# A hybrid trunk layer on one core: the state-space projection as three dense passes behind the scan

## The chip, the cores and the metric

One core of one Trainium2 chip runs the whole program in one launch. The metric is the device time in microseconds. The engines are TensorE (PE), VectorE (DVE), ScalarE (ACT), GpSimd (POOL) and SyncE (SP), which issues nearly all DMAs, in its own order. The kernel before took 2487.5 us as the median of 3 runs.

## The reference

One layer with two sub-layers runs for a prompt of 1024 tokens and for a sample group of 8 single tokens that bring caches and states; D = 1024. All numbers are float32. Cut to what matters:

```python
mod = silu(c) @ w_ada + b_ada                      # six adaLN vectors
h = rmsnorm(x) * (1 + sc1) + sh1
q, k, v, z, xbc, dt_raw, gates = split(h @ w_in)   # 3 x 768, 2048, 4096, 32, 2048 columns
attn = dilated_window_attention(q, k, v, rel_bias, caches)  # 3 groups of 4 heads of 64, merged: 256 columns
xs, B, C = split(silu(causal_conv(xbc)))           # 8 groups of 4 heads; state 128
y = chunked_scan(xs, dt, A, B, C, state) + d_skip * xs      # chunks of 128 tokens
y = y * silu(z)                                    # 2048 columns
y = y * rsqrt(mean over each group of 256 (y * y) + eps) * ssd_norm_g
g_attn, g_ssd = split(sigmoid(gates))
merged = g_attn * (attn @ w_o_attn) + g_ssd * (y @ w_o_ssd)
x = x + g1 * (merged @ w_out)
x = x + g2 * (relu(rmsnorm2(x) @ w_up) ** 2 @ w_down)       # 4096 hidden
y = rmsnorm(x)
```

The updated key and value buffers, the conv tails and the scan states of both token groups are outputs too.

## The kernel before

**Dense jobs.** The tokens (1024 + 8) lie along the free axis in three chunks of 384, 384 and 264. A `Dense` job makes 128 output columns for all three: for a chunk it runs 3 matmuls for each 128 rows of the weight (L142 to L144: high part by high, high by low, low by high), so 24 for K = 1024, into one of three `mm` PSUM buffers, and then calls an eviction. Weights come by DMA on SP (`load_raw`, L81), ACT casts the high part (L97), POOL subtracts the low one (L98), one job ahead.

**Sides.** Everything else is written as generators in a list `sides`. `run(jobs, pace)` goes on by `pace` generator steps for each chunk of a dense job (`pump`), and `rest(n)` makes a generator stay away for n dense steps. The order on PE is the order in which this program writes it; the other engines' order follows from a scheduler. `ck` tiles (19 of 384 and 10 of 264 columns) hold the scan's inputs; a dense step that finds too few free (`live`, `gated`, `CKB`) pumps the generators further first, without dense work.

**Stages.** The prologue (to about 112 us) makes the adaLN vectors (class `Mod`, L258), the transposed input (`mx` generators, L377, L382) and the first jobs' first chunks (`first_`). Attention's jobs run to about 490 us, with `bias_side` (L440 to L443: the position bias of each of the 12 heads, spread over 128 partitions by a matmul, stored to `rep_d` and read back as `bias`) and `decode_attn` (the sample tokens; values L663, transposes L674). The scan runs to about 1500 us: for each of 8 groups two `z` jobs and four `x` jobs, beside three generators of the group before (`ssd_sides`): `decode` (the sample states, L879 to L884), `chunks` and `finish_`. Of 8 chunks of 128 tokens, `load` fetches decays to `ar` (L897) and `er` (L905), `prep` transposes (L908 to L911) and scales (L916 to L926, on DVE, ACT and POOL), `state` multiplies into the state (L932), `out` makes y (L947, L951, L958). `finish_` takes a token chunk of 384: `sums` gates y by z (L969) and sums squares (L283), `rstd` is a chain of ten small DVE operations (to L233), `norm` spreads it by transposes (L982), multiplies (L985) and splits y into high and low parts, and then `project` multiplies the group's 256 columns of y with `w_o_ssd`:

```python
for f in range(8):
    ...
    for ci, (t0, nt) in enumerate(CH):
        ps = ps_mm()
        ...
        if gi == 0:
            A.copy(sacc[f][:, t0:t0 + nt], ps[:, :nt])
        else:
            V.tensor_tensor(sacc[f][:, t0:t0 + nt], ps[:, :nt], sacc[f][:, t0:t0 + nt], op=OP.add)
```

with six matmuls (L1007 to L1009) and one eviction (L1013) for a chunk. Behind the scan 16 jobs make the gates (`ga_job` to SBUF, `gs_job` multiplied into `sacc`) beside `merge` (attention's groups), 8 `oa_job`s multiply attention with `w_o_attn` (K = 256, 6 matmuls a chunk) and add both branches (L1277 makes the low part), 8 `wo_job`s apply `w_out`, and the MLP fills 1750 to 2481 us.

Of the kernel before, what the change touches and what calls it, by code (L numbers as in the profile page):

```python
# [40 lines left out]
def _trunk(ctx, tc, nc, I, O):  # L41
# [42 lines left out]
    def load_w(src, r0, kt, c0, n, side=False, into=None, raw=None):  # L84
# [128 lines left out]
    dsel = consts.tile([128, 16, 17], F32, name="dsel")  # L213

    att_d = dram.tile([3, 2, NT, 132], F32, name="att_d")
    xT_d = dram.tile([8, 128, NT], F32, name="xT_d")
    rep_d = dram.tile([12, 128, 384], F32, name="rep_d")
    qkv_d = dram.tile([3, 8, 768], F32, name="qkv_d")
    bc_d = dram.tile([8, 2, 8, 128], F32, name="bc_d")
    ac_d = dram.tile([2, 32, 1024], F32, name="ac_d")  # L220

# [13 lines left out]
    class Mod:  # L235
# [10 lines left out]
        def steps(self, slow=False):  # L246
            m = self.pool.tile([128, 512], F32, name="m4", tag="m4", bufs=1)
# [8 lines left out]
            for k in range(8):  # L256
# [6 lines left out]
                else:  # L263
                    yield
            V.tensor_copy(m[:, :256], ps[:, :256])
# [13 lines left out]
    def rstd_cols(sq, scale, eps, pool):  # L279

        ps = ps_()
        for i in range(3):
            T.matmul(ps[:, i:i + 1], sq[:, i * 128:(i + 1) * 128], ones, start=True, stop=True)  # L283
        r = pool.tile([128, 3, 3], F32, name="rstd", tag="rstd", bufs=2)
        V.tensor_scalar(r[:, 1], ps[:, :3], scale, eps, op0=OP.mult, op1=OP.add)
# [19 lines left out]
    WADA = 3  # L305
# [53 lines left out]
    def make_x(ci):  # L359
# [21 lines left out]
        for i, j in enumerate(js):  # L381
            T.transpose(rb[:, i * 128:(i + 1) * 128], rs[:, 0, j:j + 1].to_broadcast([128, 128]), ident)  # L382
        for k in range(8):
            x = xn[k, ci] = p0.tile([128, nt], F32, name="xn", tag=f"xn{ci}", bufs=8)
# [42 lines left out]
    def bias_side():  # L427
# [4 lines left out]
        for g in range(3):  # L432
            ohs.append(dp.tile([33, 384], F32, name="oh", tag="oh", bufs=2))
# [1150 lines left out]
```

## Time and profile before

| | |
|---|---|
| median of 3 runs (lowest, highest) | 2487.5 us (2484.05, 2489.03) |
| the profiled execution's own time | 2491.66 us |
| its span in the trace | 2489.9 us |
| mean granted clock of TensorE | 0.98 |
| PE busy | 2363.1 us, 95% |
| DVE, ACT, POOL busy | 1254.2, 866.6, 736.9 us |
| DMA | 254.75 MB, mean 102 GB/s |

The span goes from the first to the last instruction. Busy time is summed for each engine; a busy PE can still be slower than its best, since matmuls are pipelined and their ends are modelled. A wait is put down to the instruction that released it. PEclk is the clock that TensorE was granted, as a share of 2.4 GHz: 0.50 is 1.2 GHz.

### The profile page before, as it was taken

Reading aid. Unit: us, or ns where it says so; the run is one execution under the profiler, and the core shown is the slowest. Engines: PE = TensorE matmul, PEld = TensorE weight load, DVE = VectorE, ACT = ScalarE, POOL = GpSimd, SP = SyncE. Lnnn points to the kernel's source line nnn. Section 1 sums busy time; section 2 is a strip of 40 time slices with the busy share of each in tenths; the row PEclk is TensorE's granted clock in tenths of the full one; section 3 lists DMA queues with packets and bytes.
Section 4 is the critical chain, followed back from the end, with each engine's and each line's share of the span. In section 5 each row is a group of like instructions: output and inputs, shape, how many; then the busy total and the mean of one; then the engine's idle time right before and its main releaser. Section 6 shows DMA issues by size and latency. Waiting matters only on the chain.

```text
span 2489.9 us, 40907 instructions
## 1 busy us (share of the span) xinstructions
PE 2363.1 (95%) x15243; PEld 2245.5 (90%) x15243; DVE 1254.2 (50%) x3507; ACT 866.6 (35%) x2171; POOL 736.9 (30%) x699
## 2 busy tenths in 40 slices
PE   5999999999999999999999999989999999999998
PEld 3878898988999889989898999989999999999997
DVE  3443233677576767676767434345433333333336
ACT  4423333355543444434343312224321221221232
POOL 1112121244343434434343433343222222222230
PEclk8999999999999999999999999999999999999999
DMA  8254433343333333332333223121544544411111
GB/s 286 90 173 142 155 81 84 102 123 84 100 85 86 92 79 103 80 102 73 100 74 96 61 60 76 52 88 58 177 133 139 174 140 141 148 44 51 55 39 69
DMA packets 332482, 254.75 MB, mean 102 GB/s; under 512 B 21511, under 2 KB 323130, under 8 KB 326507
## 3 DMA queue, kind: packets, MB, share of 16 engines
q1 hardware_dynamic: 332282, 252.14, 34.8%
q8 instruction: 120, 1.97, 0.3%
q14 instruction: 80, 0.65, 0.1%
HBM read 224.50 MB, written 71.81 MB: 119 GB/s over the span
## 4 chain that ended last, share of the span: by engine, by line
PE 69%; DVE 10%; DMA 9%; issue 4%; POOL 4%; ACT 3%; SPq 1%; POOLq 0%; DVEq 0%; ACTq 0%
PE mm L142 19%; PE mm L143 19%; PE mm L144 19%; DVE ck L814 2%; DMA ar<-ac_d 2%; DMA bc<-bc_d 2%; POOL wlo L98 1%; DMA qb<-qkv_d 1%; PE ps L560 1%; DVE acc L1013 1%; DVE hst L879 1%; PE ps L951 1%; PE mm L1007 1%; DMA hst<-state_ssm 1%; PE mm L1009 1%
## 5 line engine op out<-in xcount | busy, mean ns | idle before, releaser
L142 PE MATMUL mm<-hh,whi 128*128 128x384 f32 (+4 forms) x2808 | 920.3, 328 | 7.0 <-DVE ck L814 4.7
L143 PE MATMUL mm<-hl,whi 128*128 128x384 f32 (+4 forms) x2808 | 902.2, 321 | 0.9 <-DMA xT_d<-xT 0.5
L144 PE MATMUL mm<-hh,wlo 128*128 128x384 f32 (+4 forms) x2808 | 902.2, 321 | 0.0
L98 POOL TENSOR_TENSOR wlo<-wraw,whi 128x512 fp32r<-128x512 f32 (+2 forms) x300 | 386.3, 1293 | 1022.2 <-ACT whi L97 982.6
L142 PEld LDWEIGHTS mm<-hh,whi 128*128 128x128 f32 (+1 forms) x2808 | 531.8, 189 | 14.9 <-issue 6.2
L143 PEld LDWEIGHTS mm<-hl,whi 128*128 128x128 f32 (+1 forms) x2808 | 531.0, 189 | 4.1 <-DVE hl L404 2.3
L144 PEld LDWEIGHTS mm<-hh,wlo 128*128 128x128 f32 (+1 forms) x2808 | 530.5, 189 | 1.2
L97 ACT CAST whi<-wraw 128x512 fp32r<-128x512 f32 (+2 forms) x300 | 181.4, 610 | 400.3 <-PE mm L143 318.7
L1287 DVE SCALAR_TENSOR_TENSOR acc<-mm,mod,acc 128x384 f32<-128x384 f32 (+1 forms) x216 | 123.5, 572 | 234.4 <-PE mm L144 233.4
L143 PE MATMUL mm<-dl,whi 128*128 128x384 f32 (+1 forms) x696 | 223.3, 321 | 0.0
L144 PE MATMUL mm<-dh,wlo 128*128 128x384 f32 (+1 forms) x696 | 222.3, 319 | 0.0
L142 PE MATMUL mm<-dh,whi 128*128 128x384 f32 (+1 forms) x696 | 222.3, 319 | 0.0
L814 DVE SCALAR_TENSOR_TENSOR ck<-mm,cwT,ck 128x384 f32<-128x384 f32 (+4 forms) x288 | 163.0, 567 | 66.6 <-ACT ck L810 62.9
L1374 DVE TENSOR_TENSOR r<-r 128x384 f32<-128x384 f32 (+1 forms) x96 | 69.5, 724 | 186.5 <-ACT r L1373 186.5
L1007 PE MATMUL mm<-ck,shi 128*128 128x384 f32 (+1 forms) x384 | 130.5, 340 | 23.1 <-DVE acc L1013 18.8
L926 POOL TENSOR_TENSOR ar<-ar,cb 128x512 f32<-128x512 f32 x64 | 83.4, 1303 | 161.5 <-DVE cb L921 117.4
L142 PEld LDWEIGHTS mm<-dh,whi 128*128 128x128 f32 x696 | 131.1, 188 | 0.0
L143 PEld LDWEIGHTS mm<-dl,whi 128*128 128x128 f32 x696 | 130.9, 188 | 0.0
L144 PEld LDWEIGHTS mm<-dh,wlo 128*128 128x128 f32 x696 | 130.8, 188 | 0.0
L1009 PE MATMUL mm<-ck,slo 128*128 128x384 f32 (+1 forms) x384 | 125.0, 326 | 0.6 <-POOL slo L98 0.4
L1008 PE MATMUL mm<-ck,shi 128*128 128x384 f32 (+1 forms) x384 | 124.8, 325 | 0.4 <-POOL ck L990 0.4
L923 ACT ACTIVATE ar<-ar,acs 128x128 f32<-128x128 f32 x256 | 85.3, 391 | 102.4 <-DMA ar<-ac_d 100.8
(335 smaller groups left out, 3399.8 us busy)
## 6 DMA issues: line engine op xcount, KB each, us to landing
wraw<-w_in SPq DMA_DIRECT2D x164, 256.0 KB
kv_g_sample<-cache_kv_g SPq DMA_DIRECT2D x144, 256.0 KB
wada<-w_ada SPq DMA_DIRECT2D x24, 1024.0 KB
ar<-ac_d SPq DMA_DIRECT2D x64, 256.0 KB
wraw<-w_up SPq DMA_DIRECT2D x64, 256.0 KB
wraw<-w_down SPq DMA_DIRECT2D x58, 256.0 KB
hst<-state_ssm SPq DMA_DIRECT2D x64, 128.0 KB
bc<-bc_d SPq DMA_DIRECT2D x32, 256.0 KB
```

Source lines behind the costliest of these rows:

```text
L97: A.copy(hi, raw)
L98: P.tensor_tensor(lo, raw, hi, op=OP.subtract)
L142: T.matmul(ps[:n, :m], wh, a, start=(k == 0), stop=False)
L143: T.matmul(ps[:n, :m], wh, b, start=False, stop=False)
L144: T.matmul(ps[:n, :m], wl, a, start=False, stop=(k == nk - 1))
L814: V.scalar_tensor_tensor(acc[:, o:n], ps[:, x0 + o - d:x0 + n - d], w[k], acc[:, o:n], op0=OP.mult, op1=OP.add)
L923: A.activation(ar[:, h, :], ar[:, h, :], AF.Relu, bias=acs[:, c, 4 * gi + h:4 * gi + h + 1], scale=-1.0)
L926: P.tensor_tensor(ar, ar, cb[:, None, :].to_broadcast([128, 4, 128]), op=OP.mult)
L1007: T.matmul(ps[:, :nt], hi[:, t, :], a, start=(t == 0), stop=False)
L1008: T.matmul(ps[:, :nt], hi[:, t, :], b, start=False, stop=False)
L1009: T.matmul(ps[:, :nt], lo[:, t, :], a, start=False, stop=(t == 1))
L1287: V.scalar_tensor_tensor(x[:, t0:t0 + n], ps[:, :n], gate[:, 0:1], x[:, t0:t0 + n], op0=OP.mult, op1=OP.add)
```

## The change

1. **Projection.** `project`, `rstd` and `norm` go from the scan. `gate(ci)` multiplies y by z, stores it to `y_d` (L979), and `sums` leaves the column sums in `ysum`. Behind the scan `yprep(q)` reads y back by quarters (512 columns), normalises (L1236, L1240) and splits it (L1243), and `os_job(q, f)` runs three passes of 8 jobs with K = 512, 512 and 1024; the first pass is evicted by ACT, the others add into `sacc` (L1308, L1311). In the last pass each job is followed by the `oa_job` of the same f.
2. **Chunks.** `state` and `out` of a chunk are a dense step apart, chunks are prepared three ahead and loaded four ahead, and `ar`, `er`, `xd`, `xw`, `bt`, `cb` and `hst` get more buffers.
3. **Gates.** The 16 gate jobs store their tanh to `tg_d` (L1153); five stand among the scan's `x` jobs, six at its end, five behind. `os_job` fetches the values back in its `pre`.
4. **Prologue.** `wada` gets a fourth buffer; `first_(3)` and chunk 1 of `first_(0)` go ahead of the transposes of the third token chunk, whose normalised tiles share `wada`'s memory.
5. **Bias.** Three matmuls make four rows each; a DMA stores them to `rep1_d`, and another spreads them to `rep_d`.
6. **Sample attention.** The values take 8 matmuls of 256 columns a group on four column strips (L672) in place of 16 of 4 columns; ACT and DVE copy them out, and 8 small DMAs a group collect the diagonal blocks in `u8` (L684), which the add into `so_` (L687) reads.
7. **Residual.** x1 is loaded in 8 DMAs behind the last pass, in place of a generator beside it, and the last four `w_out` jobs' weights get a pool of their own.

```diff
-    WADA = 3
+    WADA = 4
...
-        for g in range(3):
-            oh = ohs[g]
-            for h in range(4 * g, 4 * g + 4):
-                ps = ps_()
-                T.matmul(ps[:, :384], relb[:, h:h + 1].to_broadcast([33, 128]), oh, start=True, stop=True)
-                st = dp.tile([128, 384], F32, name="rep", tag="oh2", bufs=2)
-                V.tensor_copy(st, ps[:, :384])
-                dma(rep_d[h], st)
...
+        for g in range(3):
+            ps = ps_()
+            T.matmul(ps[:4, :384], relb[:, 4 * g:4 * g + 4], ohs[g], start=True, stop=True)
+            st = dp.tile([4, 384], F32, name="rep", tag="oh2", bufs=1)
+            V.tensor_copy(st, ps[:4, :384])
+            dma(rep1_d[4 * g:4 * g + 4], st)
+            dma(rep_d[4 * g:4 * g + 4], dap(rep1_d, 4 * g * 384, [[384, 4], [0, 128], [1, 384]]))
...
-            for t in range(2):
-                T.matmul(pu[:, t * 32 + b * 4:t * 32 + b * 4 + 4], vcs[b][:, t * 128:(t + 1) * 128],
-                         pd[:, b, :], start=True, stop=True)
...
+        for i in range(2):
+            for j in range(4):
+                T.matmul(pu[32 * j:32 * j + 4, 256 * i:256 * i + 256], pd[:, 4 * i + j, :], vcs[4 * i + j],
+                         start=True, stop=True)
...
+        for i in range(2):
+            for h in range(4):
+                dma(u8[4 * i:4 * i + 4, h, :], su[i].rearrange("(j r) c -> j r c", r=32)[:, h, 64 * h:64 * h + 64])
...
-            ar = D_[c] = sd.tile([128, 4, 128], F32, name="ar", tag="ar", bufs=3)
+            ar = D_[c] = sd.tile([128, 4, 128], F32, name="ar", tag="ar", bufs=5)
...
-        def sums(ci):
-            nt = CH[ci][1]
+        def gate(ci):
+            t0, nt = CH[ci]
             sq = sq_[ci] = [sd.tile([128, 384], F32, name="sq", tag="sq", bufs=2) for _ in range(2)]
             for t in range(2):
                 P.tensor_tensor(X[t][ci][:, :nt], X[t][ci][:, :nt], Z[t][ci][:, :nt], op=OP.mult)
+                dma(y_d[2 * gi + t, :, t0:t0 + nt], X[t][ci][:, :nt])
                 A.activation(sq[t][:, :nt], X[t][ci][:, :nt], AF.Square)
...
+        def sums(ci):
+            V.tensor_copy(ysum[:, gi, 3 * ci:3 * ci + 3], col_sums(sq_[ci][0]))
...
             for c in range(8):
                 state(c)
-                yield
+                yield from rest(1)
                 out(c)
-                if c + 2 < 8:
-                    prep(c + 2)
-                load(c + 3)
+                if c + 3 < 8:
+                    prep(c + 3)
+                load(c + 4)
...
-                yield from rest(1)
+                yield from rest(int(c % 3 < 2))
+                yield
...
-            yield from project()
...
+    for i in (2, 3, 0, 1, 2, 3):
+        first_(i)
...
+            if gi < 5:
+                xj.insert(2, gate_job(*gates.pop(0), sa, 3))
...
+    run([gate_job(*g, gt, GTB) for g in gates], after=os_[0][0], pace=3.0)
+    finish([preps[0], mgs])
...
+    sides.extend(preps[1:3])
+    run(os_[0], after=os_[1][0], pace=1.0)
+    finish([preps[1]])
+    sides.append(preps[3])
+    run(os_[1], after=os_[2][0], pace=1.0)
+    finish(preps[2:])
...
+    run([j for f in range(8) for j in (os_[2][f], oa_job(f))], after=wo[0])
```

Where the rows move (in the change, L140 to L142 are the dense matmuls). First DVE, before, at the start of the second group's projection (`acc<-mm` is the eviction, `hst` is a sample state, `xd` to `cb` are a chunk's preparation):

```order
L985 SCALAR_TENSOR_TENSOR ck<-ck,vecT,ps 128x264
L958 SCALAR_TENSOR_TENSOR ck<-ck,dsel,ps 128x128 x2
L916 TENSOR_TENSOR xd<-ps,dtk 128x256
L1013 TENSOR_TENSOR acc<-mm,acc 128x384
L919 TENSOR_TENSOR xw<-ps,dcy 128x256
L921 TENSOR_TENSOR cb<-ps,cst 128x128
L1013 TENSOR_TENSOR acc<-mm,acc 128x384
L879 SCALAR_TENSOR_TENSOR hst<-hst,dsel,tmp 128x128
L1013 TENSOR_TENSOR acc<-mm,acc 128x264
```

DVE in the second pass of the change (`sacc<-mm` is the eviction; `tg` holds y read back from DRAM, `yt` its low part):

```order
L1308 TENSOR_TENSOR sacc<-mm,sacc 128x384
L1243 TENSOR_TENSOR yt<-tg,yt 128x384
L1240 SCALAR_TENSOR_TENSOR tg<-tg,vecT,ps 128x384 x2
L1308 TENSOR_TENSOR sacc<-mm,sacc 128x384
L1243 TENSOR_TENSOR yt<-tg,yt 128x384 x2
L1240 SCALAR_TENSOR_TENSOR tg<-tg,vecT,ps 128x384 x2
L1308 TENSOR_TENSOR sacc<-mm,sacc 128x264
L1243 TENSOR_TENSOR yt<-tg,yt 128x384 x2
L1240 SCALAR_TENSOR_TENSOR tg<-tg,vecT,ps 128x264 x2
L1308 TENSOR_TENSOR sacc<-mm,sacc 128x384
```

The evictions stand among the scan's rows before. In the pass they stand only among the rows of `yprep`, and between two of them PE runs 12 matmuls in place of 6.

PE in the scan, before: a chunk's state, its output and the next preparation stand between two dense steps of 24 matmuls.

```order
L144 MATMUL mm<-hh,wlo 128x384
L932 MATMUL ps<-xw,bt 128x256
L947 MATMUL ps<-ck,state 128x128 x2
L951 MATMUL ps<-ar,xd 64x128 x4
L908 MATMUL ps<-cst,ck 128x128
L909 MATMUL ps<-cst,ck 128x128
L910 MATMUL ps<-cst,ck 128x128
L911 MATMUL ps<-ck 128x128
L142 MATMUL mm<-hh,whi 128x388
L143 MATMUL mm<-hl,whi 128x388
```

PE in the scan of the change, around two chunks (where rows are left out, all are matmuls of dense jobs):

```order
L142 MATMUL mm<-hh,wlo 128x384
L941 MATMUL ps<-xw,bt 128x256
L140 MATMUL mm<-hh,whi 128x388
...
L142 MATMUL mm<-hh,wlo 128x384
L956 MATMUL ps<-ck,state 128x128 x2
L960 MATMUL ps<-ar,xd 64x128 x4
L941 MATMUL ps<-xw,bt 128x256
L140 MATMUL mm<-hh,whi 128x384
```

A dense step now stands between `state` (L941) and `out` (L956, L960); here the state of the next chunk follows at once.

SP in the scan, before, at a group's end: the weights of `w_o_ssd` come among those of `w_in`.

```order
L905 DMA er<-ac_d 64x2x128 x2
L81 DMA wraw<-w_in 128x4x128 x2
L897 DMA ar<-ac_d 128x4x128 x2
L81 DMA wraw<-w_in 128x4x128 x2
L905 DMA er<-ac_d 64x2x128
L1047 DMA ssm_prompt<-fin 128x2x128
L905 DMA er<-ac_d 64x2x128 x3
L81 DMA wraw<-w_in 128x4x128
L81 DMA wraw<-w_o_ssd 128x2x128
L81 DMA wraw<-w_in 128x4x128 x2
L81 DMA wraw<-w_o_ssd 128x2x128 x2
```

SP in the scan of the change, at a group's end:

```order
L81 DMA wraw<-w_in 128x4x128 x2
L1153 DMA tg_d<-tg 128x384
L906 DMA ar<-ac_d 128x4x128
L979 DMA y_d<-ck 128x384 x2
L1153 DMA tg_d<-tg 128x384
L906 DMA ar<-ac_d 128x4x128
L81 DMA wraw<-w_in 128x4x128
L1153 DMA tg_d<-tg 128x264
L81 DMA wraw<-w_in 128x4x128
L906 DMA ar<-ac_d 128x4x128
L979 DMA y_d<-ck 128x264 x2
L81 DMA wraw<-w_in 128x4x128 x2
```

The loads of `w_o_ssd` are gone from here, and the stores of y (L979) and of the gates (L1153) stand between the weight loads, each behind its producer.

## Rows read from the trace of the kernel before

**Rows 1.** Page, part 1: span; busy us (share of the span) and instructions of each engine.

```profile
span 2489.9 us, 40907 instructions
...
PE 2363.1 (95%) x15243; PEld 2245.5 (90%) x15243; DVE 1254.2 (50%) x3507; ACT 866.6 (35%) x2171; POOL 736.9 (30%) x699
```

**Rows 2.** Stretches: window, length; busy us (count) of PE, PEld, DVE, ACT, POOL; PEclk, DMA share, GB/s.

```profile
900.00:1000.00 100.00, 94.92 (x616) 90.18 (x616) 75.28 (x224) 44.43 (x114) 39.34 (x39) 0.98 0.36 94
1800.00:1900.00 100.00, 100.00 (x639) 100.00 (x638) 33.94 (x74) 21.63 (x42) 23.24 (x18) 1.00 0.44 140
```

**Rows 3.** Waits of PE, 490 to 1600 us: line, released by; us in total, times, longest.

```profile
PE mm L1007 <- DVE acc L1013: 18.8, 22, 2.9
PE ps L982 <- DVE rstd L233: 7.0, 7, 3.5
PE ps L951 <- POOL ar L926: 6.7, 5, 2.5
...
PE ps L947 <- DVE state L938: 2.8, 2, 1.8
...
PE ps L932 <- DVE xw L919: 1.7, 1, 1.7
```

**Rows 4.** Page, part 5: the weight cast; xcount | busy, mean ns | idle before, releaser.

```profile
L97 ACT CAST whi<-wraw 128x512 fp32r<-128x512 f32 (+2 forms) x300 | 181.4, 610 | 400.3 <-PE mm L143 318.7
```

**Rows 5.** Stretches: the eight projection bursts (the fourth, the eighth, the sum).

```profile
970.80:997.90 27.10, 24.75 (x147) 22.78 (x146) 23.50 (x90) 9.80 (x29) 8.08 (x11) 1.00 0.57 164
...
1444.00:1471.50 27.50, 24.24 (x147) 22.80 (x145) 19.43 (x56) 4.50 (x13) 13.14 (x19) 1.00 0.37 97
sum 225.00, PE 200.89 PEld 186.81 DVE 179.56 ACT 82.63 POOL 71.28; mean PE 25.11 PEld 23.35 DVE 22.44 ACT 10.33 POOL 8.91
```

**Rows 6.** Groups by line, whole span: scan lines; columns as in rows 4.

```profile
L923 ACT ACTIVATE ar<-ar,acs 128x128 f32<-128x128 f32 x256 | 85.3, 391 | 102.4 <-DMA ar<-ac_d 100.8 <-POOL ar L926 1.5
L1013 DVE TENSOR_TENSOR acc<-mm,acc 128x384 f32<-128x384 f32 x168 | 84.8, 507 | 9.4 <-PE mm L1009 9.4
...
L969 POOL TENSOR_TENSOR ck<-ck 128x384 f32<-128x384 f32 (+1 forms) x48 | 47.4, 1002 | 82.3 <-DVE ck L958 81.0 <-DVE rstd L232 1.3
...
L985 DVE SCALAR_TENSOR_TENSOR ck<-ck,vecT,ps 128x384 f32<-128x384 f32 (+1 forms) x48 | 26.5, 565 | 27.6 <-PE ps L982 27.6
```

**Rows 7.** Stretch of attention's output projection; columns as in rows 2.

```profile
1603.30:1641.00 37.70, 27.42 (x147) 25.35 (x146) 25.51 (x43) 13.14 (x29) 30.02 (x29) 0.91 0.42 130
```

**Rows 8.** Waits of PE, 1600 to 1800 us; columns as in rows 3.

```profile
PE mm L142 <- DVE ck L1277: 10.1, 6, 2.4
```

**Rows 9.** Stretches of the prologue; columns as in rows 2.

```profile
16.00:20.00 4.00, 3.70 (x28) 0.67 (x27) 2.06 (x5) 0.60 (x2) 0.00 (x0) 1.00 0.69 227
68.00:74.00 6.00, 0.54 (x3) 0.33 (x3) 4.02 (x11) 6.00 (x26) 0.00 (x0) 0.77 0.00 0
76.00:81.40 5.40, 5.40 (x18) 5.38 (x19) 0.00 (x0) 0.38 (x1) 0.00 (x0) 0.50 0.34 119
```

**Rows 10.** Groups by line, 100 to 500 us; columns as in rows 4.

```profile
L258 PE MATMUL ps<-wada,cT 128*9 128x512 f32 x128 | 16.7, 595 | 1.9 <-DVE ps L253 1.9
...
L663 PE MATMUL ps<-pd,vc 128*128 128x4 f32 x96 | 11.5, 245 | 0.0
...
L440 PE MATMUL ps<-oh,relb 33*128 33x384 f32 x24 | 9.3, 508 | 0.0
...
L674 PE MATMUL ps<-cst,uT 128*8 128x128 f32 x6 | 1.3, 273 | 2.9 <-DVE uT L669 2.9
```

**Rows 11.** Timeline, 125 to 139 us, SP and DVE: start, length, engine, line [idle before].

```profile
128.75 0.91 SPq L443 DMA_DIRECT2D rep_d<-rep  x2
...
134.73 0.37 SPq L493 DMA_DIRECT2D bias<-rep_d  x1
...
137.85 0.29 DVE L538 CUSTOM_DVE_ANT_0 st<-ps,bias 128x128 f32<-128x128 f32 x1 [1.23 <-DMA bias<-rep_d]
```

**Rows 12.** Stretch of the scan; columns as in rows 2.

```profile
490.00:1400.00 910.00, 865.36 (x5712) 822.08 (x5714) 639.82 (x1880) 403.85 (x1051) 361.28 (x354) 0.99 0.35 91
```

More of the change, by code (lines that the diff above doesn't have):

```diff
@@ L277, in steps, with col_sums @@
             yield
-    def rstd_cols(sq, scale, eps, pool):
+    def col_sums(sq):
         ps = ps_()
@@ L671, in decode_attn @@
-        yield from rest(1)
-        ps = ps_()
-        for t in range(2):
-            T.transpose(ps[:8, t * 128:(t + 1) * 128], uT[:, t, :], ident)
+        yield from rest(1)
+        pu = ps_()
+        V.memset(pu, 0.0)
+        for i in range(2):
+            for j in range(4):
+                T.matmul(pu[32 * j:32 * j + 4, 256 * i:256 * i + 256], pd[:, 4 * i + j, :], vcs[4 * i + j],
+                         start=True, stop=True)
+            if i == 0:
+                for b in range(4, 8):
+                    fetch(b)
+                yield from rest(2)
@@ L1020, in chunks @@
                 yield 'wait'
-            for c in range(3):
+            for c in range(4):
                 load(c)
@@ L1054, in finish_ @@
                 yield from rest(1)
+                gate(ci)
+                yield from rest(2)
                 sums(ci)
-                yield from rest(2)
-                rstd(ci)
-                yield from rest(2)
-                norm(ci)
                 yield
-            yield from project()
         return [finish_(), chunks(), decode()]
@@ L1215, in _trunk, with yt_tiles, hl_tiles, ac_tiles @@
     V.tensor_scalar(mod[:, 16:24, :], mod[:, 16:24, :], 0.5, None, op0=OP.mult)
+    yx = [([], []) for _ in range(4)]
+    def yt_tiles():
+        return tuple([chs(yt.tile([128, NT], F32R, name="yt", tag="yt", bufs=8)) for _ in range(4)]
+                     for _ in range(2))
+    def hl_tiles():
+        return tuple([[hp_.tile([128, nt], F32R, name="yl", tag=f"hl{ci}", bufs=8)
+                       for ci, (_, nt) in enumerate(CH)] for _ in range(4)] for _ in range(2))
+    def ac_tiles():
+        t = [chs(t) for t in acc_tiles(F32R)]
+        return t[:4], t[4:]
+    def yprep(q, tiles):
+        for x, y in zip(yx[q], tiles()):
+            x.extend(y)
+        r = mg.tile([128, 3, 18], F32, name="yr", tag="yr", bufs=2)
+        V.tensor_scalar(r[:, 1], ysum[:, 2 * q:2 * q + 2, :].rearrange("p g c -> p (g c)"), 1.0 / 256, 4 * EPS,
+                        op0=OP.mult, op1=OP.add)
+        rsqrt_cols(r[:, 0], r[:, 1], r[:, 2])
+        parts = [(g, ci) for ci in range(3) for g in range(2)]
+        st = {}
+        def load(i):
+            if i < 6:
+                g, ci = parts[i]
+                t0, nt = CH[ci]
+                st[i] = []
+                for t in range(2):
+                    y = tg()
+                    dma(y[:, :nt], y_d[4 * q + 2 * g + t, :, t0:t0 + nt])
+                    st[i].append(y[:, :nt])
+        load(0)
+        load(1)
+        yield from rest(1)
+        for i, (g, ci) in enumerate(parts):
+            nt = CH[ci][1]
+            ps = ps_()
+            for k in range(3):
+                c = 9 * g + 3 * ci + k
+                T.transpose(ps[:, k * 128:(k + 1) * 128], r[:, 0, c:c + 1].to_broadcast([128, 128]), ident)
+            for t in range(2):
+                y = st[i][t]
+                c = R_SG + 4 * q + 2 * g + t
+                V.scalar_tensor_tensor(y, y, vecT[:, c:c + 1], ps[:, :nt], op0=OP.mult, op1=OP.mult)
+                hi, lo = (x[2 * g + t][ci] for x in yx[q])
+                A.copy(hi, y)
+                V.tensor_tensor(lo, y, hi, op=OP.subtract)
+            load(i + 2)
+            yield from rest(1)
     ath = [mg.tile([128, NT], F32R, name=f"ath{t}") for t in range(2)]
```

265 lines of the change are left out of this document (126 added, 139 removed).

## The prediction

> **What bounds the kernel now.** Part 1 of the page comes first: TensorE (PE) is busy 2363.1 of 2489.9 us, no other engine above half [rows 1]. Few us of plain idle are left, so I ask where PE is slower than it can be. The table by stretches gives the yardstick: in 1800 to 1900 us PE starts 639 dense matmuls in 100 us, 156.4 ns each, at the full clock; in 900 to 1000 us, inside the scan, 616, while DVE rises from 33.94 to 75.28 us [rows 2]. Then PE's waits: in the scan the largest are a projection matmul (L1007) behind its own PSUM eviction (DVE L1013, 18.8 us), the rstd transpose L982 (7.0) and the chunk products L951, L947 and L932 (6.7, 2.8, 1.7) [rows 3]. So PE bounds everything, and locally it waits for DVE or for chains of small steps. Weights are no limit: the cast L97 stands idle 318.7 us for PE to free a weight buffer [rows 4].
>
> The sum is made against the profiled execution (2491.66 us, 4.2 us above the median of 2487.5); at the end I scale by 2487.5/2491.66.
>
> **1. The projection leaves the scan.** The program pumps each group's 144 projection matmuls in one piece, so there are eight bursts, each with a PSUM eviction after only 6 matmuls. The table of the eight stretches has 225.0 us of span and 179.56 us of DVE [rows 5]. 1152 matmuls at the yardstick are 180.2 us. After, the same 1152 run as dense jobs with 12, 12 and 24 matmuls per eviction: 168 evictions by L1013 of 507 ns (84.8 us) [rows 6] become 48, and DVE has at least 1.88 us for each of 0.51. If they run at the yardstick, this gives 225.0 − 180.2 = **−44.8**. The price of the preparation that goes with it is in part 6.
>
> This needs one more thing. In the burst stretches DVE did 179.56 − 84.8 = 94.8 us of scan work, which now lies beside other matmuls. 900 to 1000 us without its burst [rows 2, 5] leaves 75.28 − 23.50 = 51.8 us of DVE in 72.9, 71%. A group's period is (1444.0 − 970.8)/4 = 118.3 us, with about 90 outside the burst; 94.8/8 = 11.9 us more there make some 84%, less the cover of the gate jobs that move into the scan and the nine small rstd operations per chunk that are gone. There is room on average, so I cost the loss of this cover at nothing; the cover is the slack of DVE, and if it fails, the second rival has the price.
>
> **2. The rest of the scan.** L982 goes (27 chains of rstd become four wider ones, outside): −7.0. State and output of a chunk, now in one PE step, are put a dense step of 24 matmuls (3.75 us) apart, chunks are prepared three ahead, and `ar` has five buffers: its exponentials waited 100.8 us for the load of `ar` [rows 6], which is what makes L926, and through it L951, late. I take two thirds of 6.7 + 2.8 + 1.7 [rows 3], −7.5; bounds 0 and −11.2. Together **−14.5**.
>
> **3. Attention's output projection.** 144 matmuls (oa) took 37.70 us, 22.5 at the yardstick; POOL is busy 30.02 and the clock 0.91 [rows 7], and PE waited 10.1 us for the operands from L1277 [rows 8]. Now each of its eight jobs stands behind a dense job of 72 matmuls (11.3 us): **−15.2**, what remains of the wait being in part 6.
>
> **4. Prologue.** 68 to 74 us holds 5.45 us of PE idle, and 18 matmuls in 76 to 81.4 us go at clock 0.50, 300 ns in place of 156.4, 2.6 us lost [rows 9]. 48 ready matmuls now stand ahead of those transposes; this goes. A fourth `wada` buffer lets the next load start earlier: in 16 to 20 us DMA moves at a share of 0.69 [rows 9], 1.26 us. **−9.3**; bounds 0 and −12.
>
> **5. Sample attention and bias.** L440 goes from 12 matmuls to 3: 9.3 us × 3/4 = −7.0. The value products L663, 11.5 us, become 24 of 256 columns on four strips; the adaLN products L258 take 16.7 us for 16 such foursomes of 512, 1.04 each [rows 10], so six of 256 take 3.1 to 6.3, I take 4: −7.5. The transposes L674 and their wait, 1.3 + 2.9 [rows 10], go: −4.2. New are two hops over DRAM or DMA. The bias now goes out and is spread by a second DMA; from issue to use the load of `bias` takes 134.73 to 137.85, 3.1 us, and its user waited 1.23 [rows 11]. PE may wait none of it or all; I take 1. The eight `u8` copies per group and the add behind them wait likewise: up to 8 × 0.45 of issue (the rate of the doubled L443 row, 0.91 for two [rows 11]) and 3.1 us of travel, 6.7 us for each of three groups. What stands behind that add on DVE is prompt attention, but PE has its dense jobs meanwhile; I take 1 each. In all **−14.7**; bounds −18.7 and +5.5.
>
> The Trainium skill ("DMA: Bandwidth & Descriptors", Anatomy of one DMA) gives a transfer some 2.0 us of fixed cost besides its bytes, for the path that GpSimd issues. This trace's 3.1 us goes with it, as the larger. By the page, eight issues and one fixed cost, 5.6 us exposed in full three times, would add some 14 us (3 × 4.6) and give about 2413.
>
> **6. New in the passes.** y goes to DRAM and back (48 pairs of transfers). Two preparations run beside pass 0; the order of PE puts their 36 transposes between six dense steps of 12 matmuls (11.3 us in all), while their 12 parts cost DVE two products like L985 (565 ns [rows 6]) and two subtractions, which I take at the same length: 2.3 us each, 27 us. Only five PSUM tiles lie between, so PE waits until some seven parts are done, 16 us and a load or two of 3.1; less the 11.3, I take 6. Eight loads of x1 stand on SP ahead of the second weight load of the output projection, 2; the eviction chain of oa, 2. **+10**; bounds 0 and +20. Gate values that are stored and fetched a job ahead (48 pairs) cost nothing: a job is 11.3 us, a load takes 3.1, and the cover is that SP is not late.
>
> **Sum:** −44.8 − 14.5 − 15.2 − 9.3 − 14.7 + 10 = −88.5; 2491.66 − 88.5 = 2403.2, and as a median **2399**.
>
> **The rivals.**
> *The gain is half given back:* the passes don't reach the yardstick (preparations, evictions in line with them) and the scan's DVE is later. Bursts −20, scan −4, attention −5, the rest as above (−15.2, −9.3, +10): −43.5, 2448, as a median 2444. For it: DVE at 84% queues. Against it: 12 matmuls per eviction.
> *Lost cover (no change):* the 94.8 us of DVE work that the bursts hid are all paid: 2403 + 95 = 2498, as a median 2494. It decides when DVE is above some 95% between chunks; the 71% speaks against it. The Trainium skill ("Perfetto Trace Analysis", Optimization Strategy) says that a kernel whose busiest engine changes over time may gain by interleaving these regimes; this change takes the projection out of the mix, and by that rule it would lose. The trace doesn't bear it out here: in the mixed bursts DVE is busy 179.56 of 225.0 us, and PE is the one that waits [rows 5].
> *SP's queue (slower):* each of the 24 pairs of stores of y waits on SP for POOL's product (L969, 1002 ns [rows 6]) and holds weight loads behind it. A job's slack is 11.3 us; where a pair's wait exceeds it, PE stops. From 88.5/24 = 3.7 us of PE for each pair the gain is gone; at 5 us the time is 2399 + 120 = 2519. Against it: the idle of L97 behind PE [rows 4].
> *More:* of 910 us of scan PE is idle in 44.6 [rows 12], 20.8 of these in its seven bursts [rows 5]. If all of the other 23.8 goes, 9.3 more than in part 2, and part 6 and the new waits of part 5 (4 us) cost nothing, it is 2403 − 23 = 2380, as a median 2376.
> *It doesn't do what it says:* no effect; against it, the order of PE shows the passes.
>
> **How the numbers follow.** Forecast 0.60, more 0.15, half 0.18, lost cover 0.03, queue 0.03, no effect 0.01. The range from 2360 to 2450 takes in the forecast with the bounds of parts 2 to 6 (a few of them at once), more and half; it leaves out the others. About 0.2% (5 us) is what a measurement of this kernel can tell from no change: faster 0.93 (the first three), same 0.03 (no effect and, as its end lies at the bound, part of lost cover), slower 0.04 (queue and the rest of lost cover).
>
> **What would show it.** Right: L1013's successor no longer among PE's waits; the three passes at 156 to 160 ns per matmul, 180 to 188 us for 1152; the scan's span from the first chunk to the last job shorter by more than 1152 × 156.4 ns; no idle at the oa jobs. Wrong: DVE above 90% through the scan with PE behind the chunk products or the convolution (then the cover was worth more than I say); SP waiting for POOL at the stores of y, with weights late; passes that start late behind the preparation; less than 5 us gained ahead of 112 us.

## The result, and the profile after

The changed kernel takes 2449.6 us (median; 2446.0 to 2452.7, four runs), the kernel before in the same rounds 2485.8: a ratio of 0.9861, 95% interval 0.9844 to 0.9878, 36 us less. The forecast was 2399, 88 us less. The two profiled executions differ by 45.7 us (spans 2489.9 and 2444.1, before rounding); the one of before was among its longer runs (over later rounds 18 runs of it lie between 2476.7 and 2491.0). Where the text compares stages it uses these two traces, elsewhere medians and ratios.

Part 1 of the page of the changed kernel, as in [rows 1]:

```profile
span 2444.1 us, 40657 instructions
...
PE 2333.1 (95%) x15171; PEld 2227.6 (91%) x15171; DVE 1191.2 (49%) x3224; ACT 861.5 (35%) x2138; POOL 686.8 (28%) x615
```

The table by stretches of the changed kernel: the scan from the first preparation of a chunk (L917) to the last chunk product (L960), and the three passes with the `oa` jobs. Columns as in [rows 2].

```profile
476.40:1282.20 805.80, 762.10 (x5103) 729.28 (x5103) 508.58 (x1469) 370.51 (x961) 300.10 (x270) 0.99 0.43 113
1382.70:1596.90 214.20, 210.84 (x1352) 209.50 (x1351) 106.37 (x199) 58.17 (x122) 69.97 (x63) 1.00 0.40 121
```

The passes are what was forecast: 1296 matmuls (1152 and 144) in 214.2 us, 202.7 at the yardstick of 156.4 ns, where bursts and `oa` took 225.0 + 37.7 [rows 5, 7]. The scan is not: PE is busy 762.10 of 805.80 us and DVE 63% of the time, less than before.

Stage by stage, from PE's first matmul on, each stage's length less its dense and projection matmuls (counted in the trace) at 156.4 ns:

```
                                              before         after       difference   forecast
start to first bias matmul                116.4-56.3     102.2-56.3       -14.2         -9.3
to the first preparation of a chunk      377.1-210.2    366.8-210.2       -10.3        -14.7
scan to the last chunk product           899.2-660.6    805.9-581.8       -14.5        -54.3
to the first oa matmul                   203.2-187.7    212.4-187.7        +9.2         +1.0
to the first w_down matmul               186.4-157.7    248.7-236.5       -16.5        -11.2
to the end                                                                 +0.6          0
```

The forecast's column is its own terms, sorted into the stages (the bursts' 44.8 with 39.8 in the scan and 5.0 behind it; of part 6, 6 to the preparations and 4 to the oa stage). Of the 42.8 us that are missing in all, the scan misses 39.8; the other stages come out nearly even. There PE waits for other things than before ([rows 3]); waits of PE and of ACT in the changed kernel's scan, columns as in [rows 3]:

```profile
PE mm L140 <- DVE ck L823: 27.0, 17, 2.8
PE ps L956 <- DVE state L947: 11.7, 6, 3.4
```

```profile
ACT ar L932 <- DMA ar<-ac_d: 128.5, 44, 6.0
```

The projection's own waits are gone, as is the rstd chain. In their place PE waits for the convolution's taps on DVE (L823; 4.7 us before) to free a PSUM buffer, and for the state (L947; 2.8 before). ACT stands 128.5 us for the loads of `ar`. It was 100.8 in a longer scan [rows 6], and two more buffers were to end it.

One such place, from the timelines of SP, ACT, DVE and PE (start, length, engine, line [idle before, released by]):

```profile
741.90 0.45 SPq L906 DMA_DIRECT2D ar<-ac_d  x1
...
743.88 0.43 ACT L832 ACTIVATE th<-ck 128x264 f32<-128x264 f32 x1
747.72 0.40 ACT L932 ACTIVATE ar<-ar,acs 128x128 f32<-128x128 f32 x1 [3.41 <-DMA ar<-ac_d]
748.02 0.24 ACT L927 COPY bt<-ps 128x128 f32<-128x128 f32 x1
748.17 0.99 ACT L932 ACTIVATE ar<-ar,acs 128x128 f32<-128x128 f32 x3
749.06 0.65 ACT L819 ACTIVATE ck<-mm,vecT,cwT 128x384 f32<-128x384 f32 x1
...
749.75 1.92 DVE L823 SCALAR_TENSOR_TENSOR ck<-mm,cwT,ck 128x381 f32<-128x381 f32 x3 [0.49 <-ACT ck L819]
...
749.56 0.60 PE L941 MATMUL ps<-xw,bt 128*128 128x256 f32 x2
751.81 0.41 PE L140 MATMUL mm<-hh,whi 128*128 128x384 f32 x1 [1.66 <-DVE ck L823]
```

SP issues the load at 741.90. ACT comes to the exponential behind it at 744.3 and stands 3.41 us until it lands. The copy `bt` and the convolution's first tap (L819), whose matmuls are long done, are queued behind it; DVE's taps (L823) wait for that one, and PE stops for 1.66 us at 751.81, since the taps hold its PSUM buffer. L932 is the first of the two steps of an exponential (L934 is the second). Its chunk is prepared three ahead, and PE uses the result at 814.6, 67 us later.

The waits for the state come by way of the sample states (`tmp` on ACT, L887, and `hst` on DVE, L888), again from the timelines of ACT and DVE:

```profile
728.78 1.28 ACT L932 ACTIVATE ar<-ar,acs 128x128 f32<-128x128 f32 x4 [4.69 <-DMA ar<-ac_d]
729.96 0.39 ACT L887 ACTIVATE tmp<-bc,dx 128x128 f32<-128x128 f32 x1
...
730.38 0.35 DVE L888 SCALAR_TENSOR_TENSOR hst<-hst,dsel,tmp 128x128 f32<-128x128 f32 x1 [3.44 <-ACT tmp L887]
...
731.46 0.42 DVE L947 TENSOR_TENSOR state<-ps,state 128x256 f32<-128x256 f32 x1
```

ACT stands 4.69 us for a load, and the next `tmp` is queued behind it. DVE's L888 waits 3.44 us for that `tmp`, the update of the state (L947) is queued behind L888, and PE's L956 starts at 732.0 after a wait of 3.16 us. All six waits for L947 stand within 1 us of the end of a group's sample states.

In the chain that ended last, from 600 to 720 us, the load of `ar` leads:

```profile
by line: DMA ar<-ac_d 24.1%; PE mm L140 9.9%; PE mm L141 9.0%; PE mm L142 9.0%; DVE ck L823 5.9%; issue 5.6%; ACT ar L932 5.1%; DVE tmp L890 3.6%; DMA bc<-bc_d 3.4%; DVE hst L888 3.2%; POOL ar L935 3.1%; POOL wlo L95 2.1%; ACT tmp L887 2.0%
```

### The profile page after: what moved, and what is told of

Read it like the earlier page. It is cut to its first block, busy times and chain, and to the rows that moved or that the text cites. A ratio compares the mean times of both kernels' runs of the same rounds, so it can differ in the third digit from the quotient of the medians.

```text
span 2444.1 us, 40657 instructions
## 1 busy us (share of the span) xinstructions
PE 2333.1 (95%) x15171; PEld 2227.6 (91%) x15171; DVE 1191.2 (49%) x3224; ACT 861.5 (35%) x2138; POOL 686.8 (28%) x615
## 4 chain that ended last, share of the span: by engine, by line
PE 70%; DMA 12%; DVE 8%; ACT 3%; issue 3%; POOL 3%; SPq 1%; DVEq 0%; ACTq 0%; POOLq 0%
PE mm L140 21%; PE mm L141 21%; PE mm L142 21%; DMA ar<-ac_d 7%; DVE ck L823 2%; ACT ar L932 1%; PE ps L571 1%; DMA wraw<-w_in 1%; POOL wlo L95 1%; DMA bc<-bc_d 1%; DVE hst L888 1%; PE ps L545 1%; POOL ar L935 1%; DVE tmp L890 1%; PE ps L562 1%
## 5 line engine op out<-in xcount | busy, mean ns | idle before, releaser
L140 PE MATMUL mm<-hh,whi 128*128 128x384 f32 (+4 forms) x2808 | 927.1, 330 | 29.8 <-DVE ck L823 27.0
L142 PE MATMUL mm<-hh,wlo 128*128 128x384 f32 (+4 forms) x2808 | 902.1, 321 | 0.0
L95 POOL TENSOR_TENSOR wlo<-wraw,whi 128x512 fp32r<-128x512 f32 (+2 forms) x332 | 425.0, 1285 | 1204.4 <-ACT whi L94 1163.7
L140 PEld LDWEIGHTS mm<-hh,whi 128*128 128x128 f32 (+1 forms) x2808 | 532.5, 190 | 45.0 <-issue 27.7
L142 PEld LDWEIGHTS mm<-hh,wlo 128*128 128x128 f32 (+1 forms) x2808 | 530.8, 189 | 1.2
L94 ACT CAST whi<-wraw 128x512 fp32r<-128x512 f32 (+2 forms) x332 | 201.4, 610 | 460.0 <-PE mm L141 393.1
L142 PE MATMUL mm<-dh,wlo 128*128 128x384 f32 (+1 forms) x696 | 222.3, 319 | 0.0
L140 PE MATMUL mm<-dh,whi 128*128 128x384 f32 (+1 forms) x696 | 222.3, 319 | 0.0
L823 DVE SCALAR_TENSOR_TENSOR ck<-mm,cwT,ck 128x384 f32<-128x384 f32 (+4 forms) x288 | 162.9, 567 | 58.2 <-ACT ck L819 54.2
L932 ACT ACTIVATE ar<-ar,acs 128x128 f32<-128x128 f32 x256 | 85.9, 393 | 129.4 <-DMA ar<-ac_d 128.5
L140 PEld LDWEIGHTS mm<-dh,whi 128*128 128x128 f32 x696 | 131.0, 188 | 0.0
L142 PEld LDWEIGHTS mm<-dh,wlo 128*128 128x128 f32 x696 | 130.8, 188 | 0.0
L888 DVE SCALAR_TENSOR_TENSOR hst<-hst,dsel,tmp 128x128 f32<-128x128 f32 x128 | 66.3, 539 | 69.0 <-ACT tmp L887 58.8
L1435 ACT ACTIVATE r<-mm 128x384 f32<-128x384 f32 (+1 forms) x96 | 43.8, 456 | 154.6 <-PE mm L142 154.1
L832 ACT ACTIVATE th<-ck 128x384 f32<-128x384 f32 (+1 forms) x96 | 47.2, 492 | 108.0 <-DVE ck L823 108.0
```

The costliest lines, as they stand in the source:

```text
L94: A.copy(hi, raw)
L95: P.tensor_tensor(lo, raw, hi, op=OP.subtract)
L140: T.matmul(ps[:n, :m], wh, a, start=(k == 0), stop=False)
L142: T.matmul(ps[:n, :m], wl, a, start=False, stop=(k == nk - 1))
L823: V.scalar_tensor_tensor(acc[:, o:n], ps[:, x0 + o - d:x0 + n - d], w[k], acc[:, o:n], op0=OP.mult, op1=OP.add)
L832: A.activation(th[:, :nt], acc[:, :nt], AF.Tanh)
```

## The experiments

The times are medians; the ratio is to the kernel before in the same rounds. Theory A: exponentials stand on ACT, in order, right behind their own loads, and hold the convolution. Theory B: the new spacing of the chunks costs the time. Theory C: the scan lacks the cover that the projection's bursts gave. Theory Q: the stores on SP's queue.

**1. The load of `ar` in a tile of its own** (changed kernel).

```diff
-            ar = D_[c] = sd.tile([128, 4, 128], F32, name="ar", tag="ar", bufs=5)
+            ar = D_[c] = sd.tile([128, 4, 128], F32, name="al", tag="al", bufs=2)
...
-            ar = D_.pop(c)
+            al = D_.pop(c)
+            ar = sd.tile([128, 4, 128], F32, name="ar", tag="ar", bufs=4)
...
-                A.activation(ar[:, h, :], ar[:, h, :], AF.Relu, bias=acs[:, c, 4 * gi + h:4 * gi + h + 1],
+                A.activation(ar[:, h, :], al[:, h, :], AF.Relu, bias=acs[:, c, 4 * gi + h:4 * gi + h + 1],
```

> The changed kernel, but the decays are loaded into a tile of their own (two buffers) and the exponentials write a second tile (four buffers), so that an exponential can't stand on ACT right behind its own load. Theory A (ACT is held in order by exponentials whose load has not landed, 128.5 us in the scan; behind them stand the first convolution tap and the z activations, and so PE's PSUM buffers): ACT's wait for the load of ar falls below 40 us, PE's wait for the taps L823 from 27.0 us to under 10, and the time falls by 15 to 30 us. Theory B (the new spacing of the chunks itself) and theory C (the bursts' cover is missing, DVE is too full): the wait of ACT goes, but the time stays within 5 us.

2391.0 us, 0.9637 (0.9619 to 0.9655): 58 us less than the changed kernel, theory A's sign at twice its size. The scan's stretch and all of PE's waits in it above 0.5 us:

```profile
480.30:1230.80 750.50, 746.73 (x5104) 721.15 (x5103) 520.47 (x1469) 377.10 (x961) 299.23 (x270) 1.00 0.46 121
```

```profile
PE ps L942 <- DVE er L966: 1.8, 1, 1.8
PE mm L140 <- DVE ysum L988: 1.2, 1, 1.2
```

The same PE instructions (x5104) take 750.5 us. PE's two named waits made 38.7 us and are gone, and the scan is 55 us shorter. Some 15 us of that is PE's busy time (762.10 to 746.73): around its stops the granted clock had fallen, to 0.69 in 730 to 735 us of the changed kernel.

**2. Part 2 undone** (chunks close together, buffers of before; changed kernel).

```diff
-                yield from rest(1)
+                yield
                 out(c)
-                if c + 3 < 8:
-                    prep(c + 3)
-                load(c + 4)
+                if c + 2 < 8:
+                    prep(c + 2)
+                load(c + 3)
```

> The changed kernel with part 2 undone: state and output of a chunk in one PE step, chunks prepared two ahead, the buffers of before. Theory A: ACT still waits about 100 us for ar, and the time changes by less than 8 us either way. Theory B (the spacing is what costs): faster by 10 us or more. The forecast's part 2 (the spacing gains 7.5): slower by about 7.

2483.2 us, 0.9994 (0.9980 to 1.0008): 34 us slower than the changed kernel, and no gain is left of the whole change. Theory B falls; theory A had expected a change of less than 8 us and the forecast's part 2 some 7 us, and both missed. The edit isn't quite part 2 undone: it leaves the four loads at a group's start, so the loop loads chunk 3 a second time (72 loads of `ar` in the trace, 64 in the others), into three buffers. Runs 7 and 12 load it twice as well. How much of the 34 us is that load's isn't known. The scan's stretch, and waits of PE and ACT in it:

```profile
477.20:1300.30 823.10, 759.59 (x4955) 720.23 (x4953) 517.79 (x1465) 370.51 (x951) 291.65 (x265) 0.96 0.42 110
```

```profile
PE ps L956 <- DVE state L947: 35.4, 17, 4.5
PE ps L941 <- DVE cb L930: 10.9, 6, 2.7
```

```profile
ACT ar L932 <- DMA ar<-ac_d: 113.9, 43, 4.6
```

ACT waits about as long as in the other kernels (113.9), but PE pays more for it: 35.4 us for the state, and the granted clock is 0.96.

**3. Parts 4 to 6 alone** (prologue, bias, sample attention in the kernel before; hunks as in the diff).

> The kernel before with parts 4 to 6 alone (prologue, bias, sample attention). The stages of the two traces give 24.5 us to them, all theories expect 20 to 28 us less than before, so about 2461; the forecast's terms said 24. If the gain of the head were lost later (the scan waits for something else), it would be under 10.

2473.4 us, 0.9959 (0.9947 to 0.9972): 12 us by the medians, where all theories had expected 20 to 28. In its trace the two stages are 20 us shorter (105.4 and 367.8), and the scan 6 longer.

**4. All gate jobs behind the scan** (changed kernel; the `xj.insert` and the six at the end taken out).

> The changed kernel with all 16 gate jobs behind the scan, as before the change. Theory C (the scan lacks PE work that covers DVE and ACT, and gate jobs are such cover): slower by 8 us or more, with more waits for L823 and L947. Theory A: the gates put their own tanh on the held ACT; without them within 5 us of the changed kernel.

2463.5 us, 0.9928 (0.9906 to 0.9951): 14 us slower than the changed kernel by the medians, 17 by the ratios. Theory C has the sign, but not its waits: PE waits 13.3 us for L823 and 6.6 for L947, less than with the gate jobs there. The granted clock of the scan is 0.96 (0.99 with them), and by stages, less dense matmuls, 7 us are lost in the scan and 7 behind it.

**5. The exponentials tied to their chunk** (kernel before), and **6. the same in the changed kernel.** One edit for both:

```diff
+            bs = sd.tile([128, 4], F32, name="bs", tag="bs", bufs=4)
+            V.scalar_tensor_tensor(bs, cb[:, :4], 0.0, acs[:, c, 4 * gi:4 * gi + 4], op0=OP.mult, op1=OP.add)
...
-                A.activation(ar[:, h, :], ar[:, h, :], AF.Relu, bias=acs[:, c, 4 * gi + h:4 * gi + h + 1],
+                A.activation(ar[:, h, :], ar[:, h, :], AF.Relu, bias=bs[:, h:h + 1],
```

> The kernel before, with the exponentials of ar tied to their own chunk: their bias is read from a small tile that DVE makes from the chunk's masked product (64 DVE operations of 4 columns more), so that ACT can't be held by a load that is only just under way. Theory A1 (the projection's bursts, which need nothing of ACT but the copies of the first group, hid the 100.8 us of waits): ACT's wait for ar goes, the time falls by less than 15 us. Theory A2 (the held ACT cost the kernel before as much as the changed one): 40 us or more faster, under 2445.

> The same edit in the changed kernel, with no other buffers than it has. If the place of the exponentials on ACT is the cause, as in the run with a tile of its own for the load, it is 40 to 60 us faster than the changed kernel, 2390 to 2410, and PE's waits for L823 and L947 nearly vanish. If the two more SBUF tiles were what helped, within 10 us of the changed kernel.

Before: 2459.0 us, 0.9913 (0.9888 to 0.9939), 24 us less, between the two cases (under 15, 40 or more). Changed: **2386.4 us**, 0.9620 (0.9602 to 0.9637), the best of all, with the buffers that the change has; so not the SBUF tiles helped in run 1 but the place of the exponentials. The scan's stretch, and ACT's group of the exponentials in it (busy, mean ns | idle before):

```profile
475.20:1220.30 745.10, 744.26 (x5104) 719.50 (x5103) 522.28 (x1533) 374.60 (x961) 299.05 (x270) 1.00 0.47 122
```

```profile
L934 ACT ACTIVATE ar<-ar,bs 128x128 f32<-128x128 f32 x256 | 81.8, 390 | 30.7 <-DVE bs L932 27.7 <-DMA ar<-ac_d 1.8 <-DMA er<-ac_d 1.1
```

PE is busy 744.26 of 745.10 us, and ACT's wait for the load is 1.8 us.

**7. Chunks close, load in a tile of its own**, and **8. gate jobs behind, load in a tile of its own** (changed kernel; edits of runs 2 and 4 with that of run 1).

> Part 2 undone (chunks close together, buffers of before), with the load of ar in a tile of its own (two and three buffers). With ACT free, what the spacing is worth by itself: theory A with the forecast's part 2 (chains of a chunk that PE waits for, some 10 us): 8 to 25 us slower than the changed kernel with the same edit, 2399 to 2416. If spacing was only a remedy for the late loads: within 6 us of it, 2385 to 2397. If the close chunks are slow for reasons of their own: above 2430.

> The changed kernel with the load of ar in a tile of its own, and all 16 gate jobs behind the scan. If gate jobs are cover that the scan needs even with a free ACT: 8 us or more slower than 2391. If they helped only against the held ACT: within 5 us of 2391.

Close: 2396.2 us, 0.9659 (0.9641 to 0.9676); with a free ACT the spacing is worth some 5 us, and the two intervals overlap. The scan's stretch and ACT's wait:

```profile
477.90:1214.50 736.60, 725.11 (x4955) 695.20 (x4953) 512.45 (x1468) 375.53 (x951) 294.68 (x266) 1.00 0.46 123
```

```profile
ACT ar L933 <- DMA al<-ac_d: 6.0, 4, 1.8
```

Gates behind: 2420.1 us, 0.9756 (0.9734 to 0.9777), 29 us slower than run 1, more than with the held ACT. The scan's stretch:

```profile
474.10:1152.20 678.10, 658.50 (x4505) 629.86 (x4503) 520.49 (x1469) 354.22 (x920) 279.54 (x254) 0.99 0.47 122
```

DVE now has 520.49 us of work in 678.1 us, 77%, and PE is busy 658.50 only; its largest waits are 7.8 us for the squares (L982) and 6.5 for `er` (L966), both on DVE. By stages 21 us are lost in the scan and 8 behind it. This part the forecast had priced at nothing.

**9. and 10. Every store of y issued twice** (changed kernel, and with tied exponentials).

```diff
                 dma(y_d[2 * gi + t, :, t0:t0 + nt], X[t][ci][:, :nt])
+                dma(y2_d[2 * gi + t, :, t0:t0 + nt], X[t][ci][:, :nt])
```

> The changed kernel with each of the 48 stores of gated y issued twice, the second to a DRAM tensor that nobody reads; the queue and its waits for POOL's product are doubled in number. The rival of the queue on SP (stores hold the loads behind them): 10 us or more slower than the changed kernel, with ACT's wait for ar above 128.5 us. Theory A (the exponentials stand too early on ACT, the queue is fast enough): within 6 us of it.

> The same doubled stores in the changed kernel with tied exponentials (2386.4). With the exponentials in their place a later load costs nothing: within 4 us of 2386. If the stores hold weight loads too: 8 us or more slower.

2448.8 us, 0.9864 (0.9848 to 0.9881), and 2387.9 us, 0.9620 (0.9606 to 0.9635): as without the second stores. ACT's wait in the first:

```profile
ACT ar L933 <- DMA ar<-ac_d: 128.8, 45, 5.8
```

Theory Q falls: SP had room.

**11. Tied exponentials and parts 4 to 6** (kernel before).

> The kernel before with tied exponentials (2459.0) and parts 4 to 6 of the change. Parts 4 to 6 alone gave 11.6 us by the medians and 20 in the stages they touch, with the scan 6 us longer. If the held ACT took the difference in the scan: 18 to 24 us faster than 2459, near 2438. If the head's gain is about 12 us in itself: near 2447.

2445.6 us, 0.9856 (0.9832 to 0.9881): 13.5 us less than run 5, near the second case. In its trace the stages of the head are 13 and 8 us shorter than in run 5's; the rest is lost behind, where the output projection's stage took 187.3 us against 181.5. The cause of that was not looked for.

**12. Chunks close, exponentials tied** (changed kernel).

> The changed kernel with part 2 undone (chunks close, buffers of before) and tied exponentials: the clean partner of the changed kernel with tied exponentials (2386.4). From the run with a tile of its own (2396.2) the spacing and its buffers should be worth 5 to 12 us with a free ACT: 2391 to 2399. Within 3 us of 2386: the spacing is worth nothing by itself. Above 2410: the tie itself costs where chunks are prepared only two ahead.

2443.6 us, 0.9852 (0.9831 to 0.9873), 47 us slower than run 7. PE's waits in the scan:

```profile
PE ps L962 <- POOL ar L937: 26.5, 22, 1.8
PE ps L958 <- DVE state L949: 17.7, 20, 2.2
```

The third case: two chunks ahead, a tied exponential comes too late for its own product. So run 5, where chunks are close too, may be only a lower bound for the kernel before, and two more runs freed its ACT otherwise.

**13. and 14. The load in a tile of its own** (kernel before; one buffer for the load and three for the exponentials, or two and three; the tail tiles 2 to 1, in run 14 the raw weight tiles 3 to 2 as well).

> The kernel before with the load of ar in a tile of its own (one buffer for the load, three for the exponentials; the tail tiles, which also hold the sample rows, go from two buffers to one to make room). Theory A1 (the projection's bursts hid the held ACT): 15 to 35 us faster than before, 2448 to 2468. Theory A2 (the held ACT cost both kernels alike): 50 us or more faster, under 2433.

> The same with two buffers for the load, as in the changed kernel's runs; the raw weight tiles go from three to two to make room, which may hold weights. Theory A1: not under 2445. Theory A2: under 2433, unless weights become PE's wait, which the trace then shows.

2456.7 us, 0.9894 (0.9876 to 0.9912), and 2462.8 us, 0.9910 (0.9888 to 0.9932): by the ratios 26 and 22 us less. ACT's wait for the load in run 13, then in run 14 with the scan's stretch:

```profile
ACT ar L924 <- DMA al<-ac_d: 69.7, 34, 5.2
```

```profile
ACT ar L924 <- PE ps L952: 28.3, 39, 1.0
...
ACT ar L924 <- DMA al<-ac_d: 1.7, 1, 1.7
```

```profile
499.80:1367.80 868.00, 842.98 (x5665) 806.69 (x5664) 627.60 (x1872) 414.67 (x1040) 361.98 (x354) 1.00 0.36 94
```

In run 13 much of the wait is still there; in run 14 it is gone (1.7 us), and still the kernel before gains no more: theory A1. The scan's stage alone is 28 and 31 us shorter than before; in run 14 the stage up to `w_down`, with fewer raw weight tiles, is 5 us longer. All runs together, as differences to before (ratio less 1, times 2485):

```
                                        ACT held   ACT free          worth of a free ACT
projection in bursts (before)               0      -26 / -22 (13, 14)        22 to 26
passes, chunks close, with the
  second load of chunk 3    (2 / 7)        -1      -85                       83
passes, chunks spread       (change / 1)  -35      -90  (tied: -94)          56 to 60
the same, gates behind      (4 / 8)       -18      -61                       43
```

## Why the prediction was right or wrong

**The failed step is in part 1**: "There is room on average, so I cost the loss of this cover at nothing". It asked whether DVE had time, by its busy share, and it did: 63% after. It didn't ask what else ran inside the bursts, and in whose queue. The scan gained 14.5 us where 54.3 were forecast.

What ran there were the sample states. From the second group on all 16 of a group's ACT steps for them (L878) stand inside a burst, 112 of 128, and with them 82 of the 87 us that ACT waits ahead of L878. In the fourth burst, 970.8 to 997.9 us of the kernel before, columns as in [rows 3]:

```profile
ACT tmp L878 <- DVE dx L875: 6.4, 4, 1.9
ACT tmp L878 <- DMA bc<-bc_d: 4.0, 2, 3.1
...
ACT ar L923 <- DMA ar<-ac_d: 0.5, 1, 0.5
```

From the second burst on these stops held no dense step, since a burst's evictions are then DVE's alone (L1013), while every other dense step of the scan is evicted through ACT first (L819, the tanh of z and of the gates). The waits for `ar` stood between the bursts (7.5 of the 100.8 us fall into them), where no sample state was queued. In the changed kernel the sample states run among dense steps, 22 to 26 us in each group from the second on; their 46 us of ACT's time and 62 us of waits (L887) stand in one queue with 128.5 us of waits for `ar` and with the evictions. From a dense step's last matmul to ACT's first reading of it the timelines have 3.1 us on average before and 5.5 after; it is above 5 us in 25 of 131 steps before, in 89 of 156 after, and there are three `mm` buffers.

The runs show that the waits for `ar` cost the changed kernel 56 to 60 us (1 and 6 against the change), and the kernel before, with its bursts, 22 to 26 (13, 14). The other parts in which the two differ don't make this: parts 4 to 6 gain 12 with ACT held and 13.5 with ACT free, without gate jobs in the scan the worth is 43, still nearly twice as much, and with close chunks it is not smaller (83, with the second load of chunk 3). So it is shown that the waits cost less with the bursts in the scan. That the place of the sample states makes the difference is read from the traces; no run moved them alone. The rival of lost cover had the sign, but not this mechanism: it asked for a DVE above 95%.

**Part 2** named the right row (L923, 100.8 us behind the load of `ar`) and drew the wrong thing from it. Five buffers didn't let the load run ahead of the exponentials; the wait grew to 128.5, since more buffers moved both forward. From the issue of a load to its first exponential the traces have 5.2 us before and 5.9 after (medians of 64 chunks), from there to PE's first use 13.6 and 53.2. The spacing gained 34 us with the held ACT (2483.2 to 2449.6, the second load of chunk 3 included) and some 5 with a free one. The L982 and L951 waits went as forecast, but the one for the state grew from 2.8 to 11.7 us. The 9.2 us behind the scan (forecast +1.0) are mostly PE's own time for the 72 transposes of the preparations, 11.4 us (nine and 1.5 us there before), which the sum left out, and their wait, 3.4 (L1236); the wait of attention's merge (L1287) was there before as well. PE's waits there:

```profile
PE ps L1287 <- issue: 4.2, 2, 3.0
PE ps L1236 <- DVE tg L1240: 3.4, 3, 1.5
PE ps L1287 <- DVE m L1280: 2.4, 2, 1.2
```

**Bursts and oa** (parts 1 and 3) were right where they ran: 48.5 us less in both together (262.7 to 214.2), forecast −60.0 + 8 (the preparations and the oa chain of part 6).

**Prologue**: −14.2 for −9.3. The stretches of the changed kernel, columns as in [rows 9]:

```profile
16.00:20.00 4.00, 3.12 (x27) 0.54 (x19) 2.79 (x6) 0.28 (x1) 0.00 (x0) 1.00 1.03 410
60.00:66.00 6.00, 6.00 (x36) 5.31 (x35) 5.69 (x13) 6.00 (x26) 0.00 (x0) 1.00 0.00 0
66.00:72.00 6.00, 6.00 (x37) 3.79 (x34) 2.93 (x14) 4.33 (x13) 0.00 (x0) 1.00 0.14 50
```

The loads of `wada` move at a share of 1.03 (0.69 before), and PE is busy through the place of the transposes, at the full clock.

**Bias and sample attention**: −10.3 for −14.7. PE's waits from 100 to 480 us, and what DVE waited for ahead of the add into `so_`:

```profile
PE ps L521 <- DVE o L549: 6.9, 3, 2.9
PE ps L545 <- DVE rep L453: 2.2, 1, 2.2
```

```profile
  DMA u<-su: 4.2, 3
```

The three waits for `u8` are 1.4 us each on DVE, and nobody waits for it: PE paid none of the 3 us that the forecast took. Some 14 us was the estimate by the fixed cost that the Trainium skill gives ("DMA: Bandwidth & Descriptors", Anatomy of one DMA), had PE paid each in full; the trace bears out no such exposure. It is the bias that PE saw, at some 5 us where the forecast took 1. One wait, 2.8 us at L521 at 133.5 us, is for the load of `bias` behind both hops. The other, 2.2 at L545, stands behind the third copy into the one `rep` buffer (two before), and that copy waits for the store of the second. DVE's rows there, from the timeline:

```profile
133.12 0.29 DVE L549 CUSTOM_DVE_ANT_0 st<-ps,bias 128x128 f32<-128x128 f32 x1 [3.22 <-DMA bias<-rep_d]
...
164.64 0.42 DVE L549 CUSTOM_DVE_ANT_0 st<-ps,bias 128x256 f32<-128x256 f32 x1 [3.12 <-DMA att_d<-o]
```

The other two at L521 (2.9 and 1.2) stand behind a store of attention's output (the second row), for which DVE waits longer than before (16.3 us in all, 9.3 before); why was not looked for.

**The rule on interleaving** of the Trainium skill ("Perfetto Trace Analysis", Optimization Strategy), which the forecast weighed as speaking against the change, is borne out in part: out of the mix, the projection took its cover along. With a free ACT the dense passes win all the same (2386.4 against 2456.7 with the bursts).

**Gates** (part 3) were priced at nothing and are worth 14 to 17 us in the changed kernel and 29 with a free ACT; of the 29, 21 are in the scan, where they put PE work between the chunks. **The queue on SP** was rightly taken as harmless. The rival that came nearest is "half given back", 2444, for a reason that it did not name. The range held the time at its very edge. The wait for `ar` stood in its own rows, and was not followed to what is queued behind it on ACT.

Small slips in the working, none of which changes the forecast by more than 1 us: "at least 1.88 us" per eviction is an average, since 12 matmuls of the 264-column chunk start within 1.5 us; of the 27 chains of rstd 24 are the projection's; and the upper bound of part 5 comes out of its own terms at +4.5 (−18.7 + 3.1 + 3 × 6.7).

## What to carry to other kernels

A busy share says whether an engine has time, not whether its queue stands: for each in-order engine, look at its longest wait and ask what is queued behind the waiting instruction and who waits for that. Before work is moved out of a stage, list what the other engines do and wait for while it runs, and look for waits in what remains: that work may have run where an engine's stops held nothing, and both then stand in one queue. More buffers can make an early consumer earlier still; give the load a tile of its own, or tie the consumer to what it belongs to.

## What the runs showed that was not expected

The two ways to free ACT are not alike: tied exponentials are the best with chunks prepared three ahead (2386.4 against 2391.0) and 47 us worse with two ahead. And short stops cost more than their sum: with chunks close, PE's two largest waits make 46 us, the granted clock of the scan is 0.96 (0.57 in 616 to 624 us, behind one such stop), and freeing ACT shortens the scan by 86.5 us (823.1 to 736.6) for the same 4955 PE instructions, 34.5 us of it in PE's busy time (759.59 to 725.11).
